# A decoder layer in three token groups: the mixing of all groups ahead of their feed-forwards, seven products for eight in each, and other group sizes

## The chip, the cores and the metric

The kernel runs on one core of a Trainium2 chip. A core has TensorE (PE; its weight loads are listed apart as PEld), VectorE (DVE), ScalarE (ACT), GpSimd (POOL) and SyncE (SP), which here issues nearly all DMA transfers. Each engine works through its own instructions in order; semaphores order them against each other. TensorE multiplies a stationary block of 128x128 weights with moving activations of up to 512 columns and accumulates in PSUM. The metric is the device time of one execution in microseconds (us), as the median of several runs. Beside them stands one profiled execution, from which all rows of the trace come.

## The reference

One layer of a hybrid decoder, for 2048 prompt tokens and 64 sample tokens (eight sequences of eight), D = 1024, in float32:

```python
h = rmsnorm(x, norm_mix_w)
proj = h @ w_in                       # 1024 x 4096: rq, rk, rv, rg, hq, hf, hi, hg, 4 heads of 128 each
o_r, s_ret = chunk_gla(rotary(rq), rotary(rk) * dk**-0.5, rv, log_gamma, s_ret)
o_h, s_hg  = chunk_gla(silu(hq) * dk**-0.5, 1 - f, hi, log(f), s_hg)     # f = lb + (1 - lb) * sigmoid(hf)
o = concat(head_rmsnorm(o_r, w) * silu(rg), head_rmsnorm(o_h, w) * silu(hg))
x = x + o @ w_out
h = rmsnorm(x, norm_ffn_w)
x = x + square(relu(h @ w_up)) @ w_down                                   # 1024 x 4096, 4096 x 1024
y = rmsnorm(x, final_norm_w)
```

`chunk_gla` is a causal gated linear recurrence; its states are outputs too. The prompt's state passes from chunk to chunk of 128 tokens, so the mixing of the prompt has an order. The feed-forward of a token depends on nothing but its own row.

## The kernel before, in words

**Numbers.** Each float32 operand of a large product is cut in two parts, hi (cast to the format that TensorE takes at full rate) and lo (the rest). A product is then three matmuls per block: hi x hi, hi x lo, lo x hi. For a weight tile (128 x 1024, 512 KB), ScalarE makes hi (L278) and VectorE or GpSimd makes lo (L293).

**Groups.** The 2112 tokens go through in three groups: 512 prompt tokens, then the 64 sample tokens with 768 prompt tokens (832), then 768. Tokens lie on the free axis: an activation is a tile of 128 features x T tokens, a "slab". There are 42 slabs of 832 columns (`sl`), 6 landing tiles for loads (`ld`), and raw, hi and lo tiles for weights (`wp`). A group of up to 512 tokens is one piece (one matmul per block), a larger one two halves (two matmuls per block).

**Mixing** (`mix`, L614, then the output projection). Per head, `project` multiplies four blocks of columns, `values` (matmuls L728) takes the values with tokens stationary, `gates` the gates; all but the values go through `proj` (matmuls L352). The recurrence of a head (`mixer`, L829) is written as a list of events on ScalarE, VectorE, GpSimd and small matmuls, placed between the matmuls of the projections. The weights of mixing and output projection are cut in the first group, and their parts stored to DRAM (`next_weight`, L318) and fetched by the other groups (`weight`, L253).

**Feed-forward.** The first group's is plain: `up_first` and `down_first` multiply all blocks, 1536 matmuls of 512 columns, and add into the residual. The other two split the two weight matrices and the tokens in halves and make seven products in place of eight (the scheme of Strassen and Winograd): `up_two` and `up` (L1472, L1521) for the first matrix, `down` (L1600) for the second, 24 matmuls of T/2 columns per product (L1176). This needs sums of weight quarters, S1 to S4, and of activation quarters, T1 to T4 (`block_sum`, L1374; its halves are cut in `halve`, L1362). The S sums are made once on VectorE (`plan_sums`, L1309; L1319), stored to DRAM and fetched like weights: those of the up matrix beside the first group's feed-forward, those of the down matrix beside the second group's mixing. The squared activations go to DRAM (`squares`, L1441) and come back as quarters in `plan_octets` (L1568). In `down`, results are added from PSUM to the residual quarters (`put`, L1610), and quarters are summed (L1377) and cut (L1366 on ScalarE, L1370 on VectorE) for the next products. An octet is seven products of one pair of weight sets, four octets make the down part.

**Order.** Group 1's mixing and feed-forward, then group 2's, then group 3's. Everything beside the large matmuls hangs on a clock of "ticks" (`tick`, L222): every large matmul or two moves it on, and `later(n, ...)` puts an operation n ticks on in the program. So the author writes the interleaving by hand, in ticks. `norm_in(nxt)` (L529), which loads the next group's tokens, weighs, cuts and squares them, runs in the last octet (or last down step) of the group before. The final norm of a group (`finish_first`, L1279; `finish`, L1683) runs beside the next group's mixing. After a group's output projection its residual quarters and norm operands stay in slabs (`out_proj`, L1340), and its operands T1 to T4 are made beside the first products (`plan_operands`, L1380).

Of the kernel before, what the change touches and what calls it, by code (L numbers as in the profile page):

```python
# [9 lines left out]
F32 = mybir.dt.float32  # L10
# [5 lines left out]
P = 128  # L16
D = 1024
# [11 lines left out]
SLAB = 832  # L29
NSLAB = 42  # L30
# [6 lines left out]
GROUPS = ((0, 0, 512), (NS, 512, 768), (0, 1280, 768))  # L37
# [4 lines left out]
W_UP0 = W_OUT0 + N_OUT  # L42
W_DN0 = W_UP0 + N_UP
NQ = FF // (4 * P)
NO = NQ // 2

W_UQ0 = W_DN0 + N_DN
W_DQ0 = W_UQ0 + N_UP
NW = W_DQ0 + N_DN

# [16 lines left out]
EARLY, LATE = (("A11", "B11"), ("A12", "B21"), ("S4", "B22")), (("S2", "T2"), ("S3", "T3"), ("S1", "T1"), ("A22", "T4"))  # L67
# [87 lines left out]
def lay_out_weights(w_in, w_out, w_up, w_down):  # L155
# [19 lines left out]
    wu = w_up.reshape(KB, P, FF // P, P)  # L175
    for f in range(FF // P):
        w[i] = wu[:, :, f].transpose(1, 0, 2).reshape(P, WT)
        i += 1
    wd = w_down.reshape(8, 4, P, 4, 256)
    for f in range(8):  # L180
        for n in range(4):
            w[i] = wd[f, :, :, n].transpose(1, 0, 2).reshape(P, WT)
            i += 1
# [25 lines left out]
class Kernel:  # L209
# [43 lines left out]
    def weight(self, i):  # L253
        n = len(self.stream)
        while self.w_next < min(i + 1 + self.ahead, n):
# [39 lines left out]
    def plan_stream(self):  # L295

        self.stream = [("w", j) for j in range(W_UP0)]
        up = [[("w", W_UP0 + 4 * t + i) for i in range(4)] for t in range(NQ)]
        dn = [[("w", W_DN0 + 4 * t + i) for i in range(4)] for t in range(NQ)]
        self.stream += up[0]  # L300
        for t in range(NQ):
            self.stream += (up[t + 1] if t < NQ - 1 else []) + dn[t]
        self.n_first = len(self.stream)
# [3 lines left out]

        for g in range(1, len(GROUPS)):
            self.stream += [("p" if j >= N_MADE else "w", j) for j in range(W_UP0)]
            for t, products in [(t, part) for part in (EARLY, LATE) for t in range(2)] + [(t, PRODUCTS) for t in range(2, NQ)]:  # L310
                self.stream += [entry(name, ("u", t), W_UQ0 + 4 * t, name in ("A12", "S1", "S4")) for name, _ in products]
            for o in range(NO):
                for k, (name, *_) in enumerate(LAST_OCTET if o == NO - 1 else OCTET):
                    end = g == len(GROUPS) - 1 and o == NO - 1 and k > 4
                    self.stream += [entry(name, ("d", o, v), W_DQ0 + 4 * (2 * o + v), not end and (2 * k + v) % 5 in (1, 3))
                                    for v in range(2)]

    def next_weight(self):  # L318
# [3 lines left out]
        if N_MADE <= i < W_UP0:  # L322
# [16 lines left out]
    def proj(self, g, blocks, acts, pieces=None):  # L339
# [3 lines left out]
        self.n_proj += 1  # L343
        if self.spread and self.n_proj % 3:
            pj = self.mm().unsqueeze(1)
        else:
            pj = self.pj.tile([P, 2, 512], F32, tag="pj", name="pj")
# [31 lines left out]
    def build(self):  # L379
        nc, tc, I = self.nc, self.tc, self.I  # L380
        with ExitStack() as ctx:
# [11 lines left out]
            self.ordered, self.spread, self.n_proj = True, False, 0  # L393
# [49 lines left out]
            for i, g in enumerate(gs):  # L443
                nxt = gs[i + 1] if i + 1 < len(gs) else None
                if i == 0:
                    self.mix(g)
                    self.plan_sums(sums[:NQ], [90 + 200 * j for j in range(NQ)])

                    self.spread = True
                    self.out_proj_first(g)  # L450
                    self.ffn_first(g, nxt)
                    self.spread = False
                    continue
                if i == 1:
                    self.finish_first(gs[0])

                    self.plan_sums(sums[NQ:], [141 + 200 * (j // 2) + 85 * (j % 2) for j in range(2 * NO)])
                else:
                    self.finish(gs[i - 1])
                self.mix(g)  # L460
                self.out_proj(g)
                while self.side:
                    self.side.popleft()[1]()
                self.ffn(g, nxt)
# [64 lines left out]
    def norm_in(self, g, start=False):  # L529
# [71 lines left out]
        else:  # L601
            for kb in range(KB):
                self.later(5 * kb, piece, kb)
        t0 = 60 if start else 5 * KB
# [576 lines left out]
    def residual(self, g):  # L1181
# [4 lines left out]
        for n in N_ORDER:  # L1186
# [4 lines left out]
        self.flush()  # L1191
        return part

    def out_proj_first(self, g):
        nc, T = self.nc, g.T
        part = self.residual(g)
        acts = g.oc[H - 1]
        g.acc, h2 = [part[n] for n in range(KB)], {}  # L1200
        for n in N_ORDER:
            pj = self.proj(g, self.take(2), acts)
            acc, hi, lo = g.acc[n], self.getr(), self.getr()
            nc.vector.tensor_tensor(out=self.v2(acc, g), in0=pj, in1=self.v2(acc, g), op=ALU.add)
            wf = self.vec[:, V_FFN + n:V_FFN + n + 1]
            nc.scalar.activation(hi[:, :T], acc[:, :T], AF.Copy, scale=wf)
            self.later(7, lambda acc=acc, hi=hi, lo=lo, wf=wf: nc.vector.scalar_tensor_tensor(
                out=lo[:, :T], in0=acc[:, :T], scalar=wf, in1=hi.bitcast(F32)[:, :T], op0=ALU.mult, op1=ALU.subtract))
            h2[n] = (hi, lo)
        g.h2 = [h2[n] for n in range(KB)]  # L1210

    def scale_residual_first(self, g):


        nc, T = self.nc, g.T
        x = {"sum": None}

        def square(acc):
            x["sum"] = self.add_square(g, x["sum"], acc)

        def split():
            x["parts"] = self.halves(g, x["sum"])

        def mean():
            x["q"] = self.get()
            for (c0, c1), ps in zip(g.pieces, self.both_sums(g, x["parts"])):
                nc.vector.tensor_scalar(out=x["q"][:, c0:c1], in0=ps, scalar1=1.0 / D, scalar2=EPS,
                                        op0=ALU.mult, op1=ALU.add)

        def scale(acc):  # L1230
            nc.gpsimd.tensor_tensor(out=acc[:, :T], in0=acc[:, :T], in1=x["q"][:, :T], op=ALU.mult)

        def guard():
            self.last_guard(g, x["q"])

        for n, acc in enumerate(g.acc):
            self.later(7 * n, square, acc)
            self.later(120 + 7 * n, scale, acc)
        self.later(92, split)
# [637 lines left out]
```

## Time and profile before

| | before |
|---|---|
| median of 3 runs | 2550.23 us (2549.39 to 2550.7) |
| profiled execution | 2551.53 us, of which the trace's span is 2548.4 us |
| granted TensorE clock | 0.999 |
| DMA traffic | 450.46 MB, mean 177 GB/s |

In the trace the stages follow one another on TensorE like this: the first group's mixing and output projection up to about 285 us, its feed-forward up to 645, the second group's mixing up to 1130 and feed-forward up to 1642, the third's up to 2063 and to the end.

A group row of the profile reads: line, engine, operation, output tile <- input tiles, shapes, how often | busy us, mean ns | idle time of the engine just before, and what ended it. A row of a stretch reads: from:to in us, its length, then for PE, PEld, DVE, ACT, POOL the busy us and the count in brackets, the granted clock, the DMA engines' share, and GB/s. Matmuls overlap in the pipeline, so what one costs is the distance from its start to the next start, not its own duration.

### The profile page before, as it was taken

How to read it: one execution, taken by the hardware profiler on the slowest of the kernel's cores; microseconds unless marked ns; L12 is line 12 of the kernel's file. 1: busy time of each engine (PE TensorE's matmuls, PEld its weight loads, DVE VectorE, ACT ScalarE, POOL GpSimd, SP SyncE). 2: the span in 40 equal slices, each digit the busy share in tenths (PEclk: the TensorE clock that was granted, in tenths of full speed). 3: DMA queues.
4: the chain of work that ended last, by engine and by line, in shares of the span. 5: the costliest groups of instructions: out<-in, count | busy, mean ns of one | idle time of the engine just before them, and what ended most of it. 6: DMA issues, size and time to landing. Idle time of an engine off the chain costs nothing. (4 is left out here: it accounts for less than half of the span.)

```text
span 2548.4 us, 37190 instructions
## 1 busy us (share of the span) xinstructions
PE 2520.3 (99%) x14635; PEld 2390.0 (94%) x14635; DVE 1712.4 (67%) x2175; ACT 1170.3 (46%) x1582; POOL 695.1 (27%) x445
## 2 busy tenths in 40 slices
PE   8999999999999999999999999999999999999998
PEld 6888888888999999999999999999999999999998
DVE  6777775457666676657646978875456466549887
ACT  6776532324434444345334444544444354345444
POOL 4333241111324243111222322243244012222220
PEclk9999999999999999999999999999999999999999
DMA  7666854556264554745457545442322335566452
GB/s 264 219 218 220 304 189 169 195 198 217 94 228 157 199 185 166 246 149 177 163 171 250 190 172 180 141 153 83 111 106 96 120 112 186 179 213 208 169 182 91
DMA packets 149342, 450.46 MB, mean 177 GB/s; under 512 B 15280, under 2 KB 37552, under 8 KB 149168
## 3 DMA queue, kind: packets, MB, share of 16 engines
q1 hardware_dynamic: 149024, 448.07, 50.8%
q8 instruction: 115, 1.88, 0.3%
q14 instruction: 59, 0.48, 0.1%
q10 hardware_dynamic: 144, 0.02, 0.0%
HBM read 336.35 MB, written 110.89 MB: 175 GB/s over the span
## 5 line engine op out<-in xcount | busy, mean ns | idle before, releaser
L352 PE MATMUL pj<-slab,hi 128*128 128x416 f32 (+2 forms) x2844 | 739.9, 363 | 7.2 <-ACT hi L278 6.1
L278 ACT CAST hi<-raw 128x1024 fp32r<-128x1024 f32 x336 | 353.3, 1052 | 677.8 <-PE pu L1176 187.8
L352 PEld LDWEIGHTS pj<-slab,hi 128*128 128x128 f32 x2844 | 513.0, 189 | 39.1 <-ACT hi L278 6.1
L293 POOL TENSOR_TENSOR lo<-raw,hi 128x1024 fp32r<-128x1024 f32 x94 | 250.9, 2670 | 842.5 <-ACT hi L278 756.1
L1176 PE MATMUL pd<-slab,hi 128*128 128x416 f32 (+1 forms) x1776 | 465.0, 342 | 2.0 <-DVE slab L1610 2.0
L352 PE MATMUL pj<-slab,lo 128*128 128x416 f32 (+2 forms) x1422 | 433.4, 363 | 0.2 <-DVE lo L293 0.2
L293 DVE TENSOR_TENSOR lo<-raw,hi 128x1024 fp32r<-128x1024 f32 x242 | 307.0, 1269 | 177.2 <-ACT hi L278 177.0
L1176 PE MATMUL pu<-slab,hi 128*128 128x416 f32 (+1 forms) x1472 | 386.0, 342 | 1.5 <-DVE slab L1370 1.5
L1176 PEld LDWEIGHTS pd<-slab,hi 128*128 128x128 f32 x1776 | 326.9, 188 | 4.9 <-issue 1.7
L1176 PE MATMUL pd<-slab,lo 128*128 128x416 f32 (+1 forms) x888 | 305.2, 344 | 0.0
L1176 PEld LDWEIGHTS pu<-slab,hi 128*128 128x128 f32 x1472 | 270.9, 188 | 4.4 <-DVE slab L1370 2.4
L352 PEld LDWEIGHTS pj<-slab,lo 128*128 128x128 f32 x1422 | 259.6, 188 | 15.6 <-DVE lo L293 0.9
L1176 PE MATMUL pu<-slab,lo 128*128 128x416 f32 (+1 forms) x736 | 252.8, 343 | 0.0
L352 PE MATMUL mm<-slab,hi 128*128 128x512 f32 x740 | 229.8, 390 | 0.0
L728 PE MATMUL pjv<-hi,slab 128*128 128x256 f32 x1088 | 212.4, 287 | 1.6 <-ACT slab L738 1.6
L1370 DVE TENSOR_TENSOR slab<-slab 128x832 fp32r<-128x832 f32 (+1 forms) x140 | 161.1, 1166 | 34.6 <-PE pd L1176 17.2
L728 PEld LDWEIGHTS pjv<-hi,slab 128*128 128x128 f32 x1088 | 174.3, 190 | 4.0 <-ACT slab L738 2.5
L1176 PEld LDWEIGHTS pd<-slab,lo 128*128 128x128 f32 x888 | 166.6, 188 | 0.5
L1366 ACT CAST slab<-slab 128x832 fp32r<-128x832 f32 (+1 forms) x140 | 118.9, 860 | 104.5 <-DVE slab L1377 72.9
L352 PEld LDWEIGHTS mm<-slab,hi 128*128 128x128 f32 x740 | 138.5, 188 | 29.1 <-ACT slab L359 0.4
L728 PE MATMUL pjv<-lo,slab 128*128 128x256 f32 x544 | 153.8, 283 | 0.0
L352 PE MATMUL mm<-slab,lo 128*128 128x512 f32 x370 | 144.4, 390 | 0.0
(223 smaller groups left out, 3752.8 us busy)
## 6 DMA issues: line engine op xcount, KB each, us to landing
raw<-w SPq DMA_DIRECT2D x272, 512.0 KB, 4.1
u<-ld SPq DMA_DIRECT2D x32, 416.0 KB, 4.1
slab<-u SPq DMA_DIRECT2D x32, 416.0 KB, 5.5
u<-ld SPq DMA_DIRECT2D x32, 384.0 KB, 4.5
slab<-u SPq DMA_DIRECT2D x32, 384.0 KB, 5.3
ld<-x SPq DMA_DIRECT2D x16, 416.0 KB, 5.9
ld<-x SPq DMA_DIRECT2D x16, 384.0 KB, 4.3
raw<-su0S SPq DMA_DIRECT2D x8, 512.0 KB, 3.2
```

The lines of the kernel that those rows point to most:

```text
L278: self.nc.scalar.copy(hi, raw)
L293: eng.tensor_tensor(out=lo, in0=self.second.pop(j), in1=hi.bitcast(F32), op=ALU.subtract)
L352: self.nc.tensor.matmul(pj[:, i, :T2], w, a[:, c0:c1], start=j == 0 and q == 0, stop=j == n - 1 and q == 2)
L728: nc.tensor.matmul(pj[:, i * 256:(i + 1) * 256], a[:, s:s + C], ww, start=kb == 0 and q == 0, stop=kb == KB - 1 and q == 2)
L1176: self.nc.tensor.matmul(*a, **k)
L1366: self.nc.scalar.copy(hi[:, :g.T], B[name][:, :g.T])
L1370: self.nc.vector.tensor_tensor(out=lo[:, :g.T], in0=B[name][:, :g.T], in1=hi.bitcast(F32)[:, :g.T], op=ALU.subtract)
```

## The change

- All three groups' mixing and output projections come first, then the three feed-forwards. In between a group's residual and its weighed copy (the feed-forward's input before the norm's factor) are kept in DRAM (`res`, `in`) and loaded back by quarters (`quarter`).
- All three feed-forwards make seven products for eight. The plain one and its functions are gone, as are the plain layouts of the two weight matrices.
- The groups have 640, 768 and 704 tokens: 640 prompt, 768 prompt, and the 64 sample tokens with the last 640. All have two pieces. There are 44 slabs of 768 columns in place of 42 of 832.
- The next group's `norm_in` runs in the output projection of the group before. `prepare` loads and cuts the operands B11, B21, B22 of a feed-forward ahead of it, for the first group in the third's output projection, for the others in the last octet of the feed-forward before. In `up_two` the two products that need B11 alone come first.
- The sums of the up matrix are made beside the second group's mixing, those of the down matrix beside the third's.
- `finish` of the first two groups runs in the up part of the next feed-forward, from tick 90 on, and the residual quarters of these feed-forwards are loaded and squared later (`wait=170`).
- Raw weights have three buffers of one kind (two before) and four of the other, filled in another alternation, and are fetched two ahead from the end of the first group's mixing on.

```diff
-SLAB = 832
-NSLAB = 42
+SLAB = 768
+NSLAB = 44
...
-GROUPS = ((0, 0, 512), (NS, 512, 768), (0, 1280, 768))
+GROUPS = ((0, 0, 640), (0, 640, 768), (NS, 1408, 640))
...
-EARLY, LATE = (("A11", "B11"), ("A12", "B21"), ("S4", "B22")), (("S2", "T2"), ("S3", "T3"), ("S1", "T1"), ("A22", "T4"))
+EARLY, LATE = (("A12", "B21"), ("S4", "B22")), (("S2", "T2"), ("S3", "T3"), ("S1", "T1"), ("A22", "T4"))
...
-            while self.w_load <= j or j >= self.n_first and self.w_load <= j + 2 and self.w_load < n:
+            while self.w_load <= j or j >= W_UQ0 and self.w_load <= j + 2 and self.w_load < n:
...
-                k, later = self.w_load, self.w_load >= self.n_first
-                raw = self.raws[k] = self.wp.tile([P, WT], F32, tag="sum" if later and k % 3 else "raw", name="raw",
-                                                  bufs=4 if later and k % 3 else 2)
+                k, later = self.w_load, self.w_load >= self.n_sums
+                other = later and k % 7 % 2
+                raw = self.raws[k] = self.wp.tile([P, WT], F32, tag="sum" if other else "raw", name="raw",
+                                                  bufs=4 if other else 3)
...
+            self.mix(gs[0])
+            self.out_proj(gs[0], 1, lambda: self.norm_in(gs[1], pace=12))
+
+            at = [141 + 192 * (j // 2) + 85 * (j % 2) for j in range(2 * H)]
+            self.plan_sums(sums[:NQ], at)
+            self.mix(gs[1])
+            self.out_proj(gs[1], 1, lambda: self.norm_in(gs[2], pace=12))
+            self.plan_sums(sums[NQ:], at)
+            self.mix(gs[2])
+            self.out_proj(gs[2], 3, lambda: self.prepare(gs[0], 12))
+            self.ffn(gs[0], lambda: self.prepare(gs[1], 8))
+            self.finish(gs[0], begin=90, pace=6, wait=180, each=8)
+            self.ffn(gs[1], lambda: self.prepare(gs[2], 8), 170)
+            self.finish(gs[1], begin=90, pace=6, wait=180, each=8)
+            self.ffn(gs[2], None, 170)
...
+    def out_proj(self, g, when, beside):
+
+        nc, T = self.nc, g.T
+        part = self.residual(g, when, beside)
+        g.res, g.in_ = (self.dp.tile([P, KB, T], F32, name=f"{name}{g.i}") for name in ("res", "in"))
         for n in N_ORDER:
...
+            pj = self.proj(g, self.take(2), g.oc[H - 1])
+            r, b = part[n], self.get()
+            nc.vector.tensor_tensor(out=self.v2(r, g), in0=pj, in1=self.v2(r, g), op=ALU.add)
+            nc.scalar.activation(b[:, :T], r[:, :T], AF.Copy, scale=self.vec[:, V_FFN + n:V_FFN + n + 1])
+            for kept, t in ((g.res, r), (g.in_, b)):
+                nc.sync.dma_start(kept[:, n], t[:, :T])
+        self.flush()
+
+    def quarter(self, g, src, v, m, h, into):
+
+        n, w = 4 * m + 2 * v, g.T // 2
+        self.nc.sync.dma_start(self.pair(g, into), src[:, n:n + 2, h * w:(h + 1) * w])
+
+    def prepare(self, g, pace):
+
+        g.B, g.ops = [{}, {}], [{}, {}]
+
+        def load(v, name):
+            g.B[v][name] = self.load()
+            self.quarter(g, g.in_, v, *PLACE[name], g.B[v][name])
+
+        for j, (name, v) in enumerate((name, v) for name in ("B11", "B21", "B22") for v in range(2)):
+            first, second = self.halve(g, g.B[v], name, g.ops[v])
+            self.later(pace * j, load, v, name)
+            self.later(pace * j + 14, first)
+            self.later(pace * j + 18, second)
...
     def plan_operands(self, g):
...
+        for v in range(2):
+            for j, name in enumerate(("B22", "B12", "B11", "B21")):
+                self.later(36 * v + 2 * j, load, v, name)
...
         for t in range(2):
-            p1, x4, z = self.get(), self.load(), {}
-            a = self.two_banks(g)
+            p1, a = self.get(), self.two_banks(g)
             self.product(g, parts(a), "B11")
             nc.scalar.copy(b2(p1), a)
+            quads.append([p1, a])
+        for t, quad in enumerate(quads):
+            a, x4, z = quad.pop(), self.get(), {}
             self.product(g, parts(a), "B21", False)
```

More of the change, by code (lines that the diff above doesn't have):

```diff
@@ L602, in norm_in @@
             for kb in range(KB):
-                self.later(5 * kb, piece, kb)
-        t0 = 60 if start else 5 * KB
+                self.later(pace * kb, piece, kb)
+        t0 = 60 if start else pace * KB
         self.later(0 if start else t0, tables)
@@ L1185, in residual @@
         part = {}
-        for n in N_ORDER:
+        for j, n in enumerate(N_ORDER):
+            if j == when:
+                beside()
             x = self.x_block(g, n)
@@ L1212, in scale_residual_first @@
[L1212 to L1239, printed above, removed]
-        self.later(112, mean)
-        self.later(194, guard)
@@ L1279, in finish_first @@
[L1279 to L1306 removed]
+        while H - 1 not in g.oc:
+            self.tick()
@@ L1681, in ffn, with finish @@
         self.flush()
-    def finish(self, g, hs=(0, 1), last=False):
+    def finish(self, g, hs=(0, 1), last=False, begin=1, pace=4, wait=51, each=5):
         nc, T, T2 = self.nc, g.T, g.T // 2
```

206 lines of the change are left out of this document (45 added, 161 removed).

## The prediction

> **What bounds the kernel now.** I read the page first (part 1, then the clock line of part 2).
>
> ```profile
> PE 2520.3 (99%) x14635; PEld 2390.0 (94%) x14635; DVE 1712.4 (67%) x2175; ACT 1170.3 (46%) x1582; POOL 695.1 (27%) x445
> PEclk9999999999999999999999999999999999999999
> ```
>
> TensorE is busy in all but 28.1 of 2548.4 us, at a clock that is not throttled. So the time is the sum of what its instructions cost, plus that idle time. A busy PE is not proof of a useful one; the waits of PE say more (us in total, times, longest; the first rows and the last of 15):
>
> ```profile
> PE pj L352 <- ACT hi L278: 6.1, 1, 6.1
> PE pd L1176 <- DVE slab L1610: 2.0, 3, 1.2
> PE pjv L728 <- ACT slab L738: 1.6, 4, 0.6
> PE pu L1176 <- DVE slab L1370: 1.5, 2, 0.8
> PE mm L1176 <- POOL lo L293: 1.3, 2, 0.9
> ...
> PE mm L887 <- DVE slab L875: 0.2, 1, 0.2
> ```
>
> The 15 add up to 18.7 us, of which 6.1 is the start; nothing else than TensorE sets the pace for long. So I price a matmul by its distance to the next one, in stretches that hold little else: busy us and count of PE per stretch (widths of 512, 416, 384 and 384 columns), then two rows of the timeline for 256.
>
> ```profile
> 400.00:600.00 200.00, 200.00 (x884) 165.60 (x883) 105.09 (x107) 59.82 (x75) 32.20 (x19) 1.00 0.52 190
> 1380.00:1560.00 180.00, 180.00 (x955) 178.35 (x954) 153.47 (x139) 82.66 (x90) 49.28 (x17) 1.00 0.57 200
> 2170.00:2300.00 130.00, 130.00 (x752) 130.00 (x751) 68.02 (x68) 54.51 (x59) 36.66 (x14) 1.00 0.61 203
> 2372.00:2500.00 128.00, 128.00 (x740) 127.98 (x739) 105.47 (x100) 53.44 (x58) 33.44 (x14) 1.00 0.51 176
> ```
>
> ```profile
> 100.13 0.40 PE L728 MATMUL pjv<-hi,slab 128*128 128x256 f32 x2
> ...
> 100.49 0.28 PE L728 MATMUL pjv<-hi,slab 128*128 128x256 f32 x1
> ```
>
> That is 200/884 = 226.2 ns for 512 columns, 180/955 = 188.5 for 416, 130/752 = 172.9 for 384, and 0.36/3 = 120 for 256 (three matmuls between the two rows). From 256 to 512 the slope is 0.415 ns a column; the line meets zero columns at about 13 ns, and 416 lies 2 ns above it. **Each matmul costs 13 to 15 ns whatever its width**, so narrower groups pay more of it.
>
> **The change, part by part.**
>
> *Matmuls.* The counts come from these two rows (the whole span, one line each):
>
> ```profile
> 0.00:2548.40 2548.40, 1173.67 (x5376) 968.73 (x5376) 1.00 0.51 177
> 0.00:2548.40 2548.40, 978.36 (x5376) 968.49 (x5376) 1.00 0.51 177
> ```
>
> L352 (first row): the mixing takes 32 weight tiles x 8 blocks x 3 = 768 matmuls a piece, the first group's plain feed-forward 64 x 8 x 3 = 1536. The 512 tokens are one piece, so 768 + 1536 = 2304 at 512 columns; the other groups have two pieces, 1536 each; the sum is 5376. L1176 (second row): seven products of 24 matmuls for 16 sets are 2688 a group. Before, then: 2304 x 226.2 = 521.2, 4224 x 188.5 = 796.2, 4224 x 172.9 = 730.3, together 2047.7 us. After, all three groups take 1536 + 2688 = 4224, at 320, 384 and 352 columns. For 320 the line gives 146.4 ns (midway between 256 and 384). For 352 it gives 159.6, and 161.6 if it carries the 2 ns of 416, which is also an odd number of 32s; I take 160.8. So 618.4 + 730.3 + 679.2 = 2027.9: **-19.8 us**. The two causes: 98,304 columns fewer (an eighth of 1536 x 512) are worth -41, and 1920 more instructions cost some 13 ns each. Bounds: -25 with 352 on the line, -10 if 320 carries the 2 ns as well and 352 all of it.
>
> The Trainium skill (TensorE: Matmul & The Clock Gate, Back-to-back issue gap) gives a warm distance of N/2.4 + 2.5 ns. By it 1920 more instructions would cost 5 us and the sum would be -36. The rows above do not bear it out: 512 columns take 226.2 ns here, not 215.8.
>
> The built program has 13 matmuls more for the column sums of the first group's norm (halves instead of one piece): +2 us at 0.15 each.
>
> *The start.* The first row is the stretch up to 8 us.
>
> ```profile
> 0.00:8.00 8.00, 1.69 (x3) 0.79 (x3) 3.61 (x14) 3.65 (x5) 1.41 (x9) 1.00 0.76 251
> ```
>
> The eight input tiles grow by 0.52 MB, 2.1 us at 251 GB/s. TensorE's own first pass grows by 1.6 us, so most of it is covered: +1, between 0 and 2.
>
> *Steps that move beside other TensorE work.* The sums S1 to S4 (64 VectorE operations) go one stage later: those of the up weights from the first feed-forward into the second group's mixing, those of the down weights into the third's. The next group's input norm goes from the last down octet into the output projection. The finish of a group goes from the next mixing into the next feed-forward. Their prices, then the stretches that take them (columns: PE, PEld, DVE, ACT, POOL busy; clock; DMA share, GB/s):
>
> ```profile
> L1319 DVE TENSOR_TENSOR raw<-raw 128x1024 f32<-128x1024 f32 x64 | 99.1, 1549 | 0.4
> ...
> L1709 DVE SCALAR_TENSOR_TENSOR slab<-slab,vec 128x416 f32<-128x416 f32 x16 | 10.8, 742 | 0.8 <-ACT slab L1743 0.8
> ...
> L543 DVE SCALAR_TENSOR_TENSOR slab<-ld,vec,slab 128x768 fp32r<-128x768 f32 x8 | 9.3, 1162 | 1.3 <-PE pd L1176 1.3
> ...
> L526 DVE TENSOR_TENSOR slab<-slab 128x768 f32<-128x768 f32 x7 | 8.6, 1226 | 0.0
> ```
>
> ```profile
> 700.00:800.00 100.00, 99.52 (x675) 97.35 (x673) 66.45 (x108) 42.39 (x66) 32.76 (x28) 1.00 0.53 180
> 1060.00:1140.00 80.00, 79.23 (x449) 77.95 (x448) 41.58 (x65) 30.08 (x46) 4.81 (x2) 1.00 0.61 201
> 1800.00:1900.00 100.00, 100.00 (x695) 98.88 (x694) 54.93 (x95) 48.15 (x69) 31.07 (x22) 1.00 0.27 99
> 2160.00:2280.00 120.00, 120.00 (x694) 120.00 (x693) 58.59 (x62) 47.42 (x51) 31.58 (x12) 1.00 0.56 182
> ```
>
> Mixing without sums keeps VectorE at 55%; half of 99 us over some 300 makes it 72%, and the row at 700 had as much with sums and lost 0.5 us in 100. The output projection is at 52% of 80 us; a norm adds some 18 (9.3 + 8.6): 75%. The up part is at 49% of 120; a finish adds some 19 (8 sums, 16 outputs). All hidden: nothing. Without that cover each would cost what it lasts, 18 to 50 us a stage.
>
> *DMA.* SP issues 1172 transfers instead of 946: 48 stores of the residual and the norm's output, 66 loads of their quarters, 64 for the first group's u, 48 more weights, about 85 MB.
>
> ```profile
> DMA packets 149342, 450.46 MB, mean 177 GB/s; under 512 B 15280, under 2 KB 37552, under 8 KB 149168
> slab<-u SPq DMA_DIRECT2D x32, 384.0 KB, 5.3
> ```
>
> 535 MB in 2540 us are 211 GB/s; the stretches above ran at 200 and 203 without a PE wait on a transfer. What is late next is a queue: SP and VectorE work in order. In each feed-forward the second half's B quarters are now loaded at ticks 36 to 42 and summed from tick 46 (ten ticks are 3 us), while such a load takes 5.3 us. VectorE stands 2 to 3 us there, the weights' lo parts queue behind it, and the finish's operations follow at tick 90. On SP a quarter's load that waits for its buffer holds up the weight fetches behind it; two prepared weights, 2 x 24 x 160.8 ns = 7.7 us of products, cover that. Now a start of this form cost 1.4 us twice (the rows L1370 and POOL lo, 2.8 in all). I put the three starts at 2.5 each: **+5**, from 0 (the 6 products before the first such sum last 21 to 25 us and hide it) to +12.
>
> *The down parts.* Durations in the stretch 2372 to 2500, VectorE and then GpSimd:
>
> ```profile
> L1610 DVE TENSOR_TENSOR slab<-pd,slab 128x768 f32<-128x768 f32 x32 | 30.3, 951 | 12.6 <-PE pd L1176 12.5
> L1370 DVE TENSOR_TENSOR slab<-slab 128x768 fp32r<-128x768 f32 x28 | 29.0, 1055 | 8.0 <-PE pd L1176 7.5 <-issue 0.3
> L293 DVE TENSOR_TENSOR lo<-raw,hi 128x1024 fp32r<-128x1024 f32 x18 | 24.4, 1355 | 0.1
> L1377 DVE TENSOR_TENSOR slab<-slab 128x768 f32<-128x768 f32 x16 | 20.4, 1302 | 1.7 <-PE pd L1176 1.7
> L1613 DVE TENSOR_TENSOR slab<-slab 128x768 f32<-128x768 f32 x6 | 7.1, 1243 | 0.0
> ```
>
> ```profile
> L293 POOL TENSOR_TENSOR lo<-raw,hi 128x1024 fp32r<-128x1024 f32 x14 | 36.1, 2575 | 100.0 <-ACT hi L278 84.0 <-DVE slab L1610 16.0
> ```
>
> The weights' 24.4 us do not shrink with the group, the other 86.8 do, and so does TensorE's 128. At 640 tokens: 72.3 + 24.4 = 97 of 108 us, 89%; at 704, 104 of 119, 87%; now 82% by busy time. Close, but below one. The step from up to down already lost 2.0 us at 384 columns and none at 416. With 2 more for the 640 group: **+2**, from 0 to +9.
>
> *Sum.* -19.8 + 2 + 1 + 5 + 2 = -9.8. The profiled execution took 2551.5 us (span 2548.4 and 3.1 around it), 1.3 above the median of the runs: 2551.5 - 9.8 - 1.3 = 2540.4, **2540**.
>
> **The rivals.** Bounds of "same" are 2545.1 and 2555.3 (0.2%, about what a measurement here can tell from no change).
>
> *The waits do not come (20%).* The operands prepared ahead and the first two products, which need B11 alone, cover the loads; VectorE keeps up. Then -19.8 + 3, or -25 + 3 with 352 on the line: 2528 to 2533. For it: no stretch of before lost over 2 us in a feed-forward.
>
> *The fixed part goes (2%).* If matmuls of 320 and 352 columns cost the slope alone, 132.8 and 146.1 ns, they would take 4224 x 28 ns = 119 us less: about 2420. All four measured widths carry the 13 ns. (The rule of the Trainium skill quoted above points this way, not as far.)
>
> *The narrow matmuls and the waits eat the gain (19%).* 320 and 352 both 2 ns dearer (-10 instead of -20), or 7 us more waits: 2545 to 2555.
>
> *GpSimd holds VectorE, and VectorE holds TensorE (13%, the slower side).* Timelines of DVE, POOL and PE in before:
>
> ```profile
> 2359.73 4.03 DVE L1377 TENSOR_TENSOR slab<-slab 128x768 f32<-128x768 f32 x2
> ...
> 2365.68 0.95 DVE L1377 TENSOR_TENSOR slab<-slab 128x768 f32<-128x768 f32 x1
> ```
>
> ```profile
> 2358.98 3.08 POOL L293 TENSOR_TENSOR lo<-raw,hi 128x1024 fp32r<-128x1024 f32 x1 [7.37 <-DVE slab L1610]
> ```
>
> ```profile
> 2364.77 0.59 PE L1176 MATMUL pd<-slab,hi 128*128 128x384 f32 x2 [1.25 <-DVE slab L1610]
> ```
>
> A sum takes 0.95 alone; two took 4.03 beside one POOL lo; 5 us later PE waited 1.25. The change adds 48 such POOL operations (94 become 142). The Trainium skill (GPSIMD Engine Reference, Key points) says that GpSimd shares its SBUF interfaces with VectorE and contends with instructions of two SBUF inputs; the trace agrees, with 4.03 against 1.9 us. A hold costs 4.03 - 1.9 = 2.1 us. It reaches PE from the point where VectorE is already more than half a product late, 24 x 146.4 ns = 3.5 us in the 640 group against 4.1 at 384. The two narrower groups have 6 holds in each of 8 octets; if every second one gets through, 24 x 2.1 = 50 us: about 2590; every third, 34 less the 7 counted: 2567. Against it: at 82% busy only three of them did.
>
> That the change does something else than it says is no rival: the built program has 4282 matmuls of 320 and 4254 of 352 columns, and none of 416.
>
> **How the numbers follow.** Forecast 2534 to 2545, 46%; the other cases as above. Faster by over 0.2%: 46 + 20 + 2 = 0.68; within: 0.19; slower: 0.13. The range 2527 to 2557 holds the first, second and fourth case, and leaves out the missing fixed part and nearly all of the slower rival.
>
> **What would show it.** The distance of matmuls in the stretches of 320 and 352 columns: 146.4 and 160.8 ns. PE's waits in the first 25 us of each feed-forward, near 2.5 us each, with VectorE (L1370's successor) as releaser. A VectorE share near 90% in the first down part and waits of PE there under 4 us; over 10 would be the slower rival. A wait of PE on a transfer, or idle time at the steps from output projection to mixing, would mean that I hid something that isn't hidden.

## The result and the profile after

The changed kernel takes **2557.25 us** (median of 5 runs, 2555.49 to 2560.66) against 2550.23 for the kernel before (5 runs, 2549.22 to 2550.7): a ratio of 1.0029, 95% interval 1.0018 to 1.0040. It is slower by 7.0 us, where the prediction had 2540 as likeliest, 0.13 for slower, and a range that ended at 2557. The profiled execution has a span of 2555.5 us, 7.1 more than before.

The page's first lines for the changed kernel (busy us, share of the span, instructions; then the DMA line):

```profile
PE 2502.8 (98%) x16569; PEld 2473.7 (97%) x16569; DVE 1848.0 (72%) x2317; ACT 1247.5 (49%) x1672; POOL 751.3 (29%) x446
DMA packets 191379, 533.81 MB, mean 209 GB/s; under 512 B 18896, under 2 KB 60112, under 8 KB 191184
```

TensorE is busy for 17.5 us less than before, near the forecast (-17.8), but it is idle for 52.7 us (2555.5 - 2502.8) where it was idle for 28.1. The closeness of the first figure is partly luck: 5.9 us of the busy time come with the waits, as the second experiment shows. The 24.6 us of new idle time are the main question. The view of PE's waits says where they are (us in total, times, longest; the first 15 of its 17 rows):

```profile
PE pd L1158 <- DVE slab L1510: 9.4, 9, 2.7
PE pd L1158 <- ACT slab L1249: 7.8, 4, 2.5
PE pj L341 <- ACT hi L268: 6.5, 1, 6.5
PE mm L488 <- DVE slab L349: 5.0, 8, 1.1
PE mm L786 <- DVE slab L783: 2.2, 4, 0.6
PE pd L1158 <- ACT hi L268: 2.1, 2, 1.1
PE pj L341 <- ACT slab L348: 1.9, 2, 1.4
PE pj L341 <- DVE slab L1174: 1.7, 1, 1.7
PE mm L548 <- DVE slab L578: 1.5, 1, 1.5
PE pu L1158 <- DVE slab L1253: 1.4, 1, 1.4
PE pu L1158 <- ACT slab L1591: 1.2, 1, 1.2
PE mm L869 <- DVE slab L857: 0.8, 1, 0.8
PE mm L1336 <- DVE slab L1328: 0.7, 1, 0.7
PE pu L1158 <- DVE slab L1377: 0.7, 2, 0.4
PE pd L1158 <- POOL lo L283: 0.5, 1, 0.5
```

The tile `pd` is the product of the down parts, and its four rows add up to 19.8 us, where before had one row of 2.0. Line L1510 is `put` (L1610 before), L1253 and L1249 are the cuts of `halve`, L283 the weights' lo. All 17 rows add up to 44.2 us, before's 15 to 18.7. By place: the start 6.5 (before 6.1); mixing and output projection 13.6 (7.8, which is 18.7 less the other three); the starts and up parts of the feed-forwards 4.3 (2.8); the down parts 19.8 (2.0). No row names a transfer.

The matmuls themselves cost what was forecast. Three stretches of the changed kernel, of 320, 384 and 352 columns (from:to, length, then busy us and count of PE, PEld, DVE, ACT, POOL, the granted clock, DMA share, GB/s):

```profile
1300.00:1400.00 100.00, 100.00 (x684) 100.00 (x683) 51.19 (x58) 44.50 (x51) 30.43 (x12) 1.00 0.66 210
1700.00:1800.00 100.00, 100.00 (x579) 100.00 (x578) 54.41 (x57) 47.79 (x53) 26.36 (x10) 1.00 0.68 222
2200.00:2300.00 100.00, 100.00 (x622) 100.00 (x622) 59.40 (x62) 46.08 (x52) 28.45 (x11) 1.00 0.64 205
```

100/684 is 146.2 ns, 100/579 is 172.7 and 100/622 is 160.8, against 146.4, 172.9 and 160.8 in the prediction. All three are up parts, VectorE is at half load and PE has no gap. In the first down part of 320 columns it looks otherwise:

```profile
1400.00:1590.00 190.00, 180.86 (x1210) 178.66 (x1209) 176.74 (x173) 97.18 (x118) 56.23 (x22) 0.99 0.66 217
```

PE misses 9 us of 190, VectorE is busy for 93% of it, GpSimd does 22 operations. One wait of the first down part in the timelines, PE first, then VectorE, then GpSimd (start, us, engine, line, operation; in brackets the idle time before and its releaser):

```profile
1449.30 0.31 PE L1158 MATMUL pd<-slab,lo 128*128 128x320 f32 x1
1451.23 0.53 PE L1158 MATMUL pd<-slab,hi 128*128 128x320 f32 x2 [1.62 <-DVE slab L1510]
1451.60 0.31 PE L1158 MATMUL pd<-slab,lo 128*128 128x320 f32 x1
```

```profile
1446.59 3.76 DVE L1253 TENSOR_TENSOR slab<-slab 128x640 fp32r<-128x640 f32 x2
1450.27 0.81 DVE L1510 TENSOR_TENSOR slab<-pd,slab 128x640 f32<-128x640 f32 x1
1451.01 1.54 DVE L1253 TENSOR_TENSOR slab<-slab 128x640 fp32r<-128x640 f32 x2
```

```profile
1447.16 2.50 POOL L283 TENSOR_TENSOR lo<-raw,hi 128x1024 fp32r<-128x1024 f32 x1 [6.38 <-ACT hi L268]
```

Read from below. GpSimd works on a weight's lo from 1447.16 to 1449.66. VectorE's two cuts take 1.54 us alone (third VectorE row) and 3.76 here: they come 2.2 us late. `put` behind them ends at 1451.08, and PE, which waits for `put` to empty its PSUM bank, starts 0.15 us later, 1.62 us after it had run dry. That VectorE was 93% busy does not yet tell whether it had too much to do or was held; the experiments ask that.

### The profile page after: what moved, and what is told of

The parts are those of the page before. It is cut to its first block, busy times and chain, and to the rows that moved or that the text cites. A ratio compares the mean times of both kernels' runs of the same rounds, so it can differ in the third digit from the quotient of the medians.

```text
span 2555.5 us, 41777 instructions
## 1 busy us (share of the span) xinstructions
PE 2502.8 (98%) x16569; PEld 2473.7 (97%) x16569; DVE 1848.0 (72%) x2317; ACT 1247.5 (49%) x1672; POOL 751.3 (29%) x446
## 2 busy tenths in 40 slices
DMA packets 191379, 533.81 MB, mean 209 GB/s; under 512 B 18896, under 2 KB 60112, under 8 KB 191184
## 4 chain that ended last, share of the span: by engine, by line
PE 78%; DVE 12%; issue 4%; ACT 3%; POOL 1%; DMA 1%; DVEq 0%; SPq 0%; ACTq 0%; POOLq 0%
PE pj L341 25%; PE pd L1158 19%; PE pu L1158 18%; PE pjv L710 4%; PE mm L1158 3%; DVE slab L1253 2%; DVE slab L1260 1%; PE mm L869 1%; DVE lo L283 1%; PE po L1049 1%; PE mm L1057 1%; PE po L1051 1%; DVE slab L1510 1%; DVE slab L349 1%; DVE slab L830 1%
## 5 line engine op out<-in xcount | busy, mean ns | idle before, releaser
L341 PE MATMUL pj<-slab,hi 128*128 128x320 f32 (+2 forms) x3072 | 661.4, 329 | 10.1 <-ACT hi L268 6.5
L283 POOL TENSOR_TENSOR lo<-raw,hi 128x1024 fp32r<-128x1024 f32 x142 | 377.1, 2656 | 987.7 <-ACT hi L268 827.2
L268 ACT CAST hi<-raw 128x1024 fp32r<-128x1024 f32 x384 | 404.0, 1053 | 533.6 <-PE pu L1158 187.7
L1158 PE MATMUL pd<-slab,hi 128*128 128x320 f32 (+2 forms) x2672 | 638.9, 323 | 19.3 <-DVE slab L1510 9.4
L1158 PE MATMUL pu<-slab,hi 128*128 128x320 f32 (+2 forms) x2208 | 527.7, 322 | 3.7 <-DVE slab L1253 1.4
L1158 PE MATMUL pd<-slab,lo 128*128 128x320 f32 (+2 forms) x1336 | 430.9, 322 | 0.5 <-POOL lo L283 0.5
L283 DVE TENSOR_TENSOR lo<-raw,hi 128x1024 fp32r<-128x1024 f32 x242 | 309.0, 1277 | 104.3 <-ACT hi L268 99.4
L341 PE MATMUL pj<-slab,lo 128*128 128x320 f32 (+2 forms) x1536 | 379.8, 328 | 0.0
L1158 PE MATMUL pu<-slab,lo 128*128 128x320 f32 (+2 forms) x1104 | 355.7, 322 | 0.0
L1253 DVE TENSOR_TENSOR slab<-slab 128x640 fp32r<-128x640 f32 (+2 forms) x192 | 234.7, 1238 | 58.4 <-ACT slab L1249 35.5
L1249 ACT CAST slab<-slab 128x640 fp32r<-128x640 f32 (+2 forms) x192 | 146.7, 781 | 141.3 <-DVE slab L1260 103.2
L1158 PEld LDWEIGHTS pu<-slab,lo 128*128 128x128 f32 x1104 | 207.1, 188 | 0.0
L1510 DVE TENSOR_TENSOR slab<-pd,slab 128x640 f32<-128x640 f32 (+2 forms) x166 | 146.1, 883 | 46.7 <-PE pd L1158 46.2
```

The lines of the kernel that those rows point to most:

```text
L268: self.nc.scalar.copy(hi, raw)
L283: eng.tensor_tensor(out=lo, in0=self.second.pop(j), in1=hi.bitcast(F32), op=ALU.subtract)
L341: self.nc.tensor.matmul(pj[:, i, :T2], w, a[:, c0:c1], start=j == 0 and q == 0, stop=j == n - 1 and q == 2)
L1158: self.nc.tensor.matmul(*a, **k)
L1249: self.nc.scalar.copy(hi[:, :g.T], B[name][:, :g.T])
L1253: self.nc.vector.tensor_tensor(out=lo[:, :g.T], in0=B[name][:, :g.T], in1=hi.bitcast(F32)[:, :g.T], op=ALU.subtract)
```

## The experiments

The expectations call the theories by short names. **HOLD**: a two-input operation of VectorE stands still while GpSimd makes a lo, and at 320 columns these holds reach PE. **LOAD**: VectorE has too much work of its own in a down part that is shorter by a sixth than at 384 columns, whatever GpSimd does. **SUMS**: the weight sums are not hidden in the mixing. Others are said where they stand. Each ratio is taken against runs of the kernel before made beside the experiment: 2550.29 us for the first four experiments, 2550.42 for the other four. The changed kernel's 2557.25 us is from its own runs, beside 2550.23; the three figures for the kernel before differ by 0.2 us at most.

**No GpSimd in the down parts, copies on ScalarE.** The 70 lo parts that GpSimd makes in the down parts become copies on ScalarE. This kernel leaves the subtraction of these parts out, so it does not compute the reference; it serves for its time alone.

```diff
             pool = len(self.stream[j]) > 2 and self.stream[j][2]
-            if pool or j < 4:
+            if pool == "act":
+                self.nc.scalar.copy(lo, self.second.pop(j))
+            elif pool or j < 4:
...
-                                          not (end and o == NO - 1 and k > 4) and (2 * k + v) % 5 in (1, 3)) for v in range(2)]
+                                          "act" if not (end and o == NO - 1 and k > 4) and (2 * k + v) % 5 in (1, 3) else False) for v in range(2)]
```

> In the three down parts the 70 lo parts of weights that GpSimd makes are written by ScalarE as plain copies of the raw weight (left out: the subtraction). VectorE's own work is as in the changed kernel, but no GpSimd operation lies beside it. Theory HOLD (a GpSimd operation holds VectorE's two-input operations, and that makes VectorE late for TensorE): TensorE's waits in the down parts fall from 19.8 us to under 5 and the time from 2557 to about 2542. Rival LOAD (VectorE's own work, whose weights' part does not shrink with the group, is too much at 320 columns, with or without GpSimd): the waits stay above 15 us and the time within 4 us of 2557. Rival PLACE (what runs beside the first feed-forward, wherever its width): no change either.

Measured: 2530.91 us (2529.6 to 2534.05), ratio 0.9925 (0.9912 to 0.9939). The view of PE's waits has no `pd` row at all, so the waits behind ScalarE (L1249, L268) are gone too, although ScalarE has 63 us more to do (1310.9 busy, 1247.5 before the edit). They were the tail of VectorE's lateness, not ScalarE's own. The time fell by 26 us, where some 15 were expected.

**The same work on VectorE.** This tests LOAD from the other side: VectorE, already at 93%, gets the 70 operations as well.

```diff
-                                          not (end and o == NO - 1 and k > 4) and (2 * k + v) % 5 in (1, 3)) for v in range(2)]
+                                          False) for v in range(2)]
```

> The same 70 lo parts are made by VectorE, so it has 6 operations of 1.2 us more in each octet and no GpSimd beside it. HOLD: a hold costs about 2.1 us and the operation itself 1.1, so the waits in the down parts fall from 19.8 us to some 6 to 10, time 2545 to 2549. LOAD: VectorE's work rises by 7 us in an octet of 49; the waits rise above 30 us, time over 2567. PLACE: the waits change little in the second and third down part.

Measured: 2531.81 us (2530.27 to 2533.0), ratio 0.9927 (0.9914 to 0.9939); again no `pd` row. The same stretch of this kernel:

```profile
1400.00:1590.00 190.00, 190.00 (x1298) 190.00 (x1297) 178.53 (x206) 100.04 (x121) 3.85 (x2) 1.00 0.70 233
```

VectorE is as busy as it was (178.53 us against 176.74), with 206 operations in place of 173, and PE does not wait. The groups of VectorE show why. First the changed kernel's, in its stretch 1400 to 1590, then this kernel's, 1400 to 1580 (count, busy us, mean ns, idle before):

```profile
L1253 DVE TENSOR_TENSOR slab<-slab 128x640 fp32r<-128x640 f32 x54 | 65.0, 1222 | 8.8 <-PE pd L1158 5.9 <-ACT slab L1249 2.4
L1260 DVE TENSOR_TENSOR slab<-slab 128x640 f32<-128x640 f32 x32 | 39.2, 1240 | 0.1
L1510 DVE TENSOR_TENSOR slab<-pd,slab 128x640 f32<-128x640 f32 x46 | 37.3, 815 | 1.3 <-PE pd L1158 1.2
L283 DVE TENSOR_TENSOR lo<-raw,hi 128x1024 fp32r<-128x1024 f32 x29 | 35.2, 1213 | 4.9 <-ACT hi L268 4.9
```

```profile
L283 DVE TENSOR_TENSOR lo<-raw,hi 128x1024 fp32r<-128x1024 f32 x50 | 60.9, 1219 | 7.7 <-ACT hi L268 7.0
L1253 DVE TENSOR_TENSOR slab<-slab 128x640 fp32r<-128x640 f32 x54 | 45.5, 857 | 0.0
L1510 DVE TENSOR_TENSOR slab<-pd,slab 128x640 f32<-128x640 f32 x46 | 37.5, 819 | 4.4 <-PE pd L1158 3.6
L1260 DVE TENSOR_TENSOR slab<-slab 128x640 f32<-128x640 f32 x32 | 25.3, 816 | 0.0
```

The cuts (L1253) and the sums (L1260), which read both inputs from SBUF, lose 54 x 365 + 32 x 424 ns = 33 us of the stretch to holds; `put`, which reads one input from PSUM, loses nothing (815 and 819 ns). The timelines of VectorE and GpSimd, laid side by side, show it operation by operation: in the changed kernel the 33 cuts and 24 sums that overlap no GpSimd operation take 0.81 to 0.82 us on average, the 21 cuts and 8 sums that do overlap one take 1.86 and 2.52. VectorE's own lo parts (L283) read two SBUF inputs as well, but only 4 of the 29 overlap a GpSimd operation, each by less than 1 us, and their mean does not change. Own work was 176.7 - 33.3 = 143 us, 75%. LOAD falls, since VectorE is as busy as before and nothing waits; HOLD stands, though its own figures for this kernel (6 to 10 us of waits, 2545 to 2549 us) were too high: no wait is left. The Trainium skill (SBUF — State Buffer, Who interferes with whom) says that a VectorE instruction with two SBUF inputs contends with a GpSimd instruction that reads SBUF, and that one with at most one SBUF input, outside the two-port modes, does not. The trace agrees on both, with these means.

The gain, 25.4 us, is more than the 19.8 us of waits. In the spans it is 24.8, of which PE's idle time makes 18.9 (52.7 to 33.8) and its busy time 5.9 (2502.8 to 2496.9). A wait costs more than its row: in the timeline above, 1.93 us lie between the starts at 1449.30 and 1451.23, so 1.78 are lost where the row has 1.62, and the two matmuls after the wait take 0.37 in place of 0.29. That is 0.24 us beyond the row. Worked out in the same way, the other `pd` waits of over 0.2 us give 0.23 to 0.27, so 16 waits make 3.8 us; a dip of the clock (last section) makes 1.7 more.

**The 768 group's feed-forward first.** The first down part might be slow for its place, ahead of all others, and not for its width. The order of the feed-forwards becomes 768, 640, 704.

```diff
-            self.out_proj(gs[2], 3, lambda: self.prepare(gs[0], 12))
-            self.ffn(gs[0], lambda: self.prepare(gs[1], 8))
-            self.finish(gs[0], begin=90, pace=6, wait=180, each=8)
-            self.ffn(gs[1], lambda: self.prepare(gs[2], 8), 170)
+            self.out_proj(gs[2], 3, lambda: self.prepare(gs[1], 12))
+            self.ffn(gs[1], lambda: self.prepare(gs[0], 8))
             self.finish(gs[1], begin=90, pace=6, wait=180, each=8)
+            self.ffn(gs[0], lambda: self.prepare(gs[2], 8), 170)
+            self.finish(gs[0], begin=90, pace=6, wait=180, each=8)
             self.ffn(gs[2], None, 170)
```

> Only the order of the feed-forwards changes: 768, 640, 704 tokens. HOLD and LOAD, which both go by width: the 640 group keeps its 12 us of waits in its down part, now the second, and the 768 group its 2 to 3, now the first; time within 4 us of 2557. PLACE: the first down part has the 12 us, now at 384 columns, and the second 3 or less.

Measured: 2568.05 us (2564.47 to 2570.88), ratio 1.0069 (1.0055 to 1.0082). PE's waits in the second feed-forward, now the one of 320 columns (1660 to 2100 us, the first five of seven rows):

```profile
PE pd L1158 <- DVE slab L1510: 6.7, 6, 1.9
PE pd L1158 <- ACT slab L1249: 3.6, 2, 1.8
PE pu L1158 <- DVE slab L1437: 3.5, 1, 3.5
PE mm L1336 <- DVE slab L1328: 1.9, 2, 1.1
PE pd L1158 <- ACT hi L268: 1.0, 1, 1.0
```

The `pd` waits of the 640 group moved with it, 11.3 us here and 11.9 in the first place, while the 768 group in the first place has 2.4: the width decides, as HOLD and LOAD both say, and PLACE falls. The time missed its expectation by some 7 us. Two things in the trace go with it; their shares were not separated. The up part of 320 columns now has the finish of a 768 group beside it (the rows L1437 and L1328), and the granted clock dips five times, not once (mean 0.995, 0.998 in the changed kernel).

**GpSimd's lo parts kept.** In the order of the kernel above, the lo parts that GpSimd makes in the first down part are stored to DRAM and fetched in the other two, which trades 46 GpSimd operations (446 become 400) for 36.7 MB of transfers. The main lines of the edit:

```diff
+            if pool == "kept" and self.stream[j][1] in self.lows:
+                self.nc.sync.dma_start(lo.bitcast(F32), self.lows[self.stream[j][1]])
+                self.w_next += 1
+                continue
...
+        if len(x) > 2 and x[2] == "kept" and x[1] not in self.lows:
+            low = self.lows[x[1]] = self.dp.tile([P, WT], F32, name=f"low{i}")
+            self.nc.sync.dma_start(low, r[1].bitcast(F32))
```

> Order 768, 640, 704; in the first down part the lo parts that GpSimd makes are also stored to DRAM, and the two others fetch them (some 46 transfers of 512 KB) where GpSimd made them. HOLD: waits in the down parts of 640 and 704 fall from 17 us together to under 6, time about 2545, which would beat both kernels. LOAD: they stay, time 2557 or more. A third way: the added transfers (about 0.07 MB per us more) come late, which would show as waits of TensorE on lo by DMA.

Measured: 2545.68 us (11 runs, 2541.9 to 2549.27), ratio 0.9979 (0.9971 to 0.9988), as expected. `pd` waits are 2.4 us in all, every one in the first down part, where GpSimd still makes its lo parts; those of the up part stay (the longest row is L1445 here, 3.5 us). Against its own base, 2568.05, this is 22 us less; the transfers came in time. So it is GpSimd's running at that moment that costs, and not that these lo parts are needed.

**Every second GpSimd operation.** The share of the down weights that goes to GpSimd is halved, 70 to 35. (In the expectation, e2 is the experiment that gives the same work to VectorE.)

```diff
-                                          not (end and o == NO - 1 and k > 4) and (2 * k + v) % 5 in (1, 3)) for v in range(2)]
+                                          not (end and o == NO - 1 and k > 4) and (2 * k + v) % 5 == 3) for v in range(2)]
```

> The changed kernel with half the dose: GpSimd makes 3 of the 14 lo parts of an octet instead of 6, VectorE the others. HOLD: the waits in the down parts lie between 19.8 us (six) and 0 (none), and below the middle, since a queue that is rarely late forgives a hold: 2 to 8 us; time 2534 to 2543. Rival THRESHOLD by VectorE's work alone does not fit e2 any more and is not expected.

Measured: 2535.75 us (2533.36 to 2537.28), ratio 0.9942 (0.9928 to 0.9955), as expected. One `pd` row is left:

```profile
PE pd L1158 <- DVE slab L1510: 4.7, 5, 1.7
```

With 70, 35 and 0 operations the waits are 19.8, 4.7 and 0 us, and the times 2557, 2536 and 2532. The first 35 operations bring 4.7 us of waits, the next 35 another 15.1: the cost is not in proportion. A likely reading is that a hold by itself is mostly made up before PE notices, and two close together are not. The traces bear it out in part. In the changed kernel's down parts of 320 and 352 columns, nine GpSimd operations start 5.3 to 7.0 us after the one before, and the six longest `pd` waits (1.7 to 2.7 us) come 4 to 7 us after six of these nine. But in the kernel with half of them, where most stand 13 to 23 us apart, one that started 16 us after the one before was still followed by a wait of 1.7 us. No experiment moved the distance alone.

**The kernel before without its own.** The 46 lo parts that GpSimd makes in before's down parts (416 and 384 columns) go to VectorE.

```diff
-                    self.stream += [entry(name, ("d", o, v), W_DQ0 + 4 * (2 * o + v), not end and (2 * k + v) % 5 in (1, 3))
+                    self.stream += [entry(name, ("d", o, v), W_DQ0 + 4 * (2 * o + v), False)
```

> The kernel before, with the lo parts of its two down parts made by VectorE instead of GpSimd. HOLD, as sized here: at 416 and 384 columns the holds cost it only the 2.0 us that it waits there, so 2548 (from 2550.2). Then the change by itself, without holds, is worth 2531.8 - 2548 = -16, as its matmuls are. Rival LAYOUT: the gain seen comes from something that the wide kernel would have gained as well (below 2540).

Measured: 2548.09 us (11 runs, 2546.36 to 2549.33), ratio 0.9989 (0.9981 to 0.9998). As expected: the same split of work that costs the changed kernel 25 us costs this one 2.3 (2550.42 - 2548.09). With the holds out of both, the change is worth 2531.81 - 2548.09 = -16.3 us.

**No weight sums.** On the version with no GpSimd in the down parts, the products take plain quarters, and S1 to S4 are not made. This kernel leaves the sums out, so it does not compute the reference either.

```diff
-            return ("s", key + (name,), pool) if name[0] == "S" else ("w", i0 + A_PLACE[name], pool)
+            return ("w", i0 + A_PLACE.get(name, int(name[1]) - 1), pool)
...
-            self.plan_sums(sums[:NQ], at)
-            self.plan_sums(sums[NQ:], at)
```

> On the kernel without GpSimd in its down parts (2531.8 us): the sums S1 to S4 are not made; the products take plain weight quarters in their place (left out: 64 additions of VectorE in the mixing of the second and third group, their loads and stores). The waits of the mixing stages are 11.3 us there against 7.6 in the kernel before. Theory SUMS (moving the sums into mixing wasn't free): they fall by 4 us or more, time 2526 to 2528. Rival WIDTH (shorter products leave the mixing's chains less cover, with or without sums): they stay above 9, time 2530 to 2532.

Measured: 2523.06 us (2520.89 to 2523.35), ratio 0.9891 (0.9878 to 0.9905): 8.8 less than with the sums, where 4 to 6 were expected. Its waits come to 15.9 us, against 25.1. In the mixing, the row of the norm's column sums falls from 4.2 to 1.1 us, and L783, 2.1, and L1174, 2.1, are gone. The rows of the kernel with sums, then the one that is left without them:

```profile
PE mm L488 <- DVE slab L349: 4.2, 5, 1.1
PE mm L786 <- DVE slab L783: 2.1, 4, 0.6
PE pj L341 <- DVE slab L1174: 2.1, 1, 2.1
```

```profile
PE mm L486 <- DVE slab L349: 1.1, 1, 1.1
```

SUMS holds, and WIDTH falls: the waits of the mixing come to 6.3 us, where WIDTH named 9 or more. Of the 9.2 us, 2.3 lie at the feed-forwards' products and the rest nearly all in the mixing. The sums' loads and stores are left out too, so that it is VectorE's additions and not these 67 MB that cost is read from the order of VectorE's operations (next section), not from a run of its own.

**No GpSimd in the feed-forwards at all.** The up weights' lo parts go from GpSimd to VectorE too.

```diff
-                self.stream += [entry(name, ("u", t), W_UQ0 + 4 * t, name in ("A12", "S1", "S4")) for name, _ in products]
+                self.stream += [entry(name, ("u", t), W_UQ0 + 4 * t, False) for name, _ in products]
...
-                                          not (end and o == NO - 1 and k > 4) and (2 * k + v) % 5 in (1, 3)) for v in range(2)]
+                                          False) for v in range(2)]
```

> On top of the kernel whose down parts have no GpSimd (2531.8 us), VectorE makes the 72 lo parts of the up parts too; GpSimd has no work left in the feed-forwards. HOLD: the up parts have room (VectorE at 50 to 70%), but at their starts VectorE is the late engine; 3 operations in 7 more there cost 1.1 us each and save holds of about 2. The waits there, 5.5 us now, fall to 3 to 5; time 2529 to 2532. If VectorE's own work matters at the starts, they rise to 8 or more; time 2535.

Measured: **2526.66 us** (2524.79 to 2528.37), ratio 0.9908 (0.9893 to 0.9923), below the expectation. It leaves nothing of the reference out, and it is faster than both kernels. The waits of the feed-forwards that are left:

```profile
PE mm L1158 <- DVE lo L283: 1.2, 1, 1.2
PE mm L1158 <- ACT hi L268: 0.3, 1, 0.3
```

GpSimd is idle in the second half of the kernel, and VectorE is busy for 74% of the span.

## Why the prediction was wrong, step by step

- **Matmuls, -19.8: right.** Busy time of PE on the two lines of large matmuls (whole span). The kernel before without GpSimd in the down parts, then the changed one without it:

```profile
0.00:2545.50 2545.50, 1173.64 (x5376) 1.00 0.52 177
0.00:2545.50 2545.50, 977.35 (x5376) 1.00 0.52 177
```

```profile
0.00:2530.70 2530.70, 1296.34 (x8064) 1.00 0.62 211
0.00:2530.70 2530.70, 835.02 (x4608) 1.00 0.62 211
```

  2131.4 - 2151.0 = -19.6 us. The rival with the fixed part gone falls, and so does the one with dearer narrow matmuls. (The upper bound of this term, -10, was added up wrongly: 2 ns more at 320 columns and 0.8 at 352 on 4224 matmuls each make -8. The rival of dearer narrow matmuls quotes it too; its range of 2545 to 2555 holds either.)
- **13 matmuls for column sums, +2: not seen.** PE's other busy time went from 368.3 (2519.3 in all) to 365.5 us (2496.9 in all), 2.8 less. Where these come from is open.
- **Start, +1: about right**, 0.4. **Starts of the feed-forwards, +5: too high**, 1.5 (2.8 to 4.3). **DMA: right**, 533.81 MB at 209 GB/s, and PE waits on no transfer.
- **Sums and other steps hidden, nothing: mis-sized.** The waits of mixing and output projection rose by 5.8 us, and the experiment without sums gives back 8.8. The share of VectorE, 72% by my working, said that there was room on average. But PE waits in order for some of VectorE's operations there: the cut ahead of a norm's column sums (L349), the sample tokens' values (L783), the first addition to the residual (L1174). A sum that stands ahead of one on VectorE delays it. In the trace a sum of 1.2 us runs two operations ahead of the cut at each of the three waits of L488 between 500 and 680 us, 1.0 us each. For L1174, where no sum stands close ahead, the link is not shown. What the same sums cost in the kernel before was not tried.
- **Down parts, +2 within 0 to +9: the step that failed.** The waits rose by 17.8 us, and with what comes after a wait the GpSimd operations there cost 25.4. My 97 of 108 us scaled busy times of before (1055 and 1302 ns), in which holds were already mixed with work, and compared a sum with a sum. It also set 89% against 82%, which is another measure: the same rows of before add up to 111.2 of 128 us, 87%. VectorE's own work is 75% of that part; what decided was when single operations came late, which no share of busy time shows.
- **"GpSimd holds VectorE, and VectorE holds TensorE", 13%: the mechanism that occurred**, and the list of what would show it named it (over 10 us). Its price per hold was right (2.1 us; 2.2 in the timeline). The direction of its point of decision fits too: half a product (24 matmuls) is 3.5 us at 320 columns, 4.1 at 384, and in the changed kernel the `pd` waits are 11.9 us in the 640 group, 5.5 at 352 columns and 2.5 at 384. That the threshold lies at half a product was not measured. How many get through was the error in the other direction: 16 waits behind 70 operations, 1.2 us on average, so a hold is partly made up on the way.
- **The sum.** With no holds, -19.6 for the large matmuls, -2.8 for the others and +8.4 for the waits (16.7 to 25.1) make -14.0; the two spans differ by -14.8, the medians by -16.3. Then holds of +25.4, against 2.3 in before: -16.3 + 25.4 - 2.3 = +6.8, and +7.0 was measured. The last line only adds up differences of the same medians; that they close is no further evidence.

I had seen the right row, 4.03 us for two sums beside one GpSimd operation, and weighed it by how seldom such a hold reached PE at 416 and 384 columns. The change made exactly that cover shorter.

## What to carry to other kernels

A narrower product shortens the cover of every delay whose length does not depend on the width: set the holds that can follow one another on the engine that empties PSUM (here up to 2.2 us each, 5 to 15 us apart) against the time in which they can be made up, not its busy share against the whole. A busy share that contains holds is not all work: measure an operation's mean where the other engine is idle. Work that was handed to GpSimd to relieve VectorE can cost more VectorE time than it saves (1848.0 us busy with it, 1843.6 without); here, taking it back at 93% busy made the kernel faster by 25 us.

## What the runs showed of the hardware

A short wait inside a dense stream of matmuls can be followed by a lower granted clock. In the changed kernel, a wait of 1.92 us, and one of 2.66 us:

```profile
1572.52 0.53 PE L1158 MATMUL pd<-slab,hi 128*128 128x320 f32 x2 [1.92 <-DVE slab L1510]
...
1601.72 0.53 PE L1158 MATMUL pd<-slab,hi 128*128 128x320 f32 x2 [2.66 <-DVE slab L1510]
```

The stretches of 10 us around them, and the dip in the first of them by itself (the clock is the third number from the end):

```profile
1570.00:1580.00 10.00, 8.09 (x46) 7.85 (x45) 7.49 (x8) 4.83 (x6) 2.09 (x2) 0.83 0.64 218
1600.00:1610.00 10.00, 8.28 (x56) 8.31 (x57) 8.50 (x10) 2.16 (x3) 0.00 (x0) 1.00 0.49 131
1573.47:1576.88 3.41, 3.41 (x15) 3.41 (x14) 2.83 (x3) 3.41 (x5) 0.00 (x0) 0.50 0.22 53
```

The dip is 3.41 us at half speed, 1.7 us lost, and it begins 0.95 us after the end of the wait. The longer wait brought no dip, so its length alone does not decide. The Trainium skill (TensorE: Matmul & The Clock Gate, What's actually happening) knows two rates, half and full, and a free-running window of about 3.4 us; the dip agrees with both, but the page ties a drop to an idle window of that length, and the wait here was 1.92 us. The kernel with the 768 group first has five such dips (one of them 6.83 us long), the one with the down parts' GpSimd work on VectorE none before its end. In the four profiles that have dips in the middle of the kernel, nine in all, each begins during a wait of PE of 1.1 us or more, or within 2.3 us of its end. The spread of the changed kernel's runs, 5.2 us against 1.5 before, goes the same way: the two runs of 2560 us have a mean clock of 0.997, the two of 2555.5 to 2556.0 one of 0.999. That the waits cause the dips is not shown by a run of its own.
